# Two chained transformer blocks on one core: weight buffers in order of last use, later expert additions, and a softmax with negated minima whose division runs on GpSimd

## The chip, the cores and the metric

The kernel runs on one core of one Trainium2 chip. The metric is device microseconds (us) of one execution. Before the change the median of three runs was 2263.86 us (2260.80 to 2268.84).

Names of engines in the profile: PE is TensorE (matmul), PEld its weight load, DVE VectorE, ACT ScalarE, POOL GpSimd, SP the engine whose queue issues the weight transfers.

## The reference

`T` = 256 tokens of width 1024, float32. Block 1 has two layers of a mixer and an expert-choice FFN; block 2 has a token mixer (a gated linear recurrence and a long convolution) and a hierarchical mixture of 32 experts. What the change touches is block 1:

```python
def banked_softmax(s, sink):                  # s: scores + ALiBi bias + mask, per head
    m = max(s, axis=-1); m = maximum(m, sink) # sink only in the window attention
    p = exp(s - m)
    den = sum(p, axis=-1) + exp(sink - m)
    return (p / den) @ v

def hybrid_mixer(h):     # proj = h @ w_in; dilated: 4 heads x 3 dilations, window: 16 heads, 4 of keys
    g = sigmoid(gates + b_gate)
    return (g[0] * (dilated(q, k, v) @ w_a) + g[1] * (window(q, k, v, sink) @ w_b)) @ w_out

def expert_choice_ffn(h):                     # 16 experts, each takes its 32 best tokens
    aff = softmax(h @ w_router); gate, idx = top_k(aff.T, 32)
    ye = (silu(h[idx] @ w_gate) * (h[idx] @ w_up)) @ w_down
    return zeros.at[idx].add(gate * ye)
```

(Condensed; the dilated part combines its three dilations by their softmax denominators, which is one softmax over the concatenated 512 scores.)

## The kernel before

**Weights.** 745.8 MB of weights come from HBM, nearly all as chunks of 128 partitions x 2048 float32, 1 MB each. `Core.chunk` (L45) takes the next tag and `piece` (L57, DMA at L60) issues the transfer on SP into a buffer of that tag; `quarters` (L68) does it as four tiles of 512 columns. The tags are `w` (5 buffers), `x` (4 buffers), and the tiles of activations that are idle in that stage (`V`, `qa`, `qb`, `qc`, `ob`, `hgw`, `G`, `hn`, `hTa`). A fixed list, `K.ring`, with a running counter sets which tag is next; a list `K.spare` is used up ahead of it. SP issues in order, and a transfer waits until the last reader of its buffer is through. The compiler's scheduler fixes the order of instructions on each engine from the order in the program and its own model of time.

**Projections.** Matmuls of block 1's mixers and of block 2's token mixer are done as three passes (`mm3`, L118 to L120) over a high and a low part. `split` (L98, L99) makes them of a chunk's 512 columns: ACT copies the high part `wh`, then `wl` = chunk - `wh` is computed by DVE, or by POOL for every fourth. Layer 1's input projections but a last quarter are computed early, beside layer 0's expert down projections (class `Ahead`, whose generator `steps` gives 23 steps for each quarter of the model's width). Layer 1's mixer then has the last quarter of its projections (`pairs`, `rows`, added at L242), and the attention.

**Attention** (`mixer`, L318 on). For each head of a pair, the scores go to PSUM (`sc`, L436 dilated, L477 and L478 window), and DVE adds slope times distance and takes the running maximum (`ttr`, L423). `soften` (L405 to L420) negates the maximum (`nm`, L408, DVE), takes the exponential with the sum `den` (L411, ACT), adds the sink's term (L414 to L416), takes the reciprocal `r` (L418, DVE) and multiplies the probabilities `P` by it (L420, DVE). Then four transposes (L446, L484), a copy to `PT`, and the products with V (L454, L493). `P` and `PT` have four buffers each. `weave` interleaves these items with the projections: with `project_w` the dilated part, with the gates and the adaptive-norm products (`ada`, L565) the window part. `split_to` (L106, L107) writes the window output `ob`. The gates `Ga`, `Gb` are multiplied on POOL in layer 1 (L383).

**Experts** (L681 on). The router, the choice of tokens and a gather come first; then 16 experts' gate and up products (L774, 8 chunks each), and in four quarters `q` of the width, for four groups `y` of experts, the down products (L816, 4 chunks), the scaling `yd` (L109, L110), and the addition to `h`: four matmuls (L824) with the scatter matrix `Ge` and one DVE addition (L827). In layer 0, `ahead.steps` follow each addition from the second quarter on; in layer 1 pieces of `prep` (constants of block 2) stand between.

Of the kernel before, what the change touches and what calls it, by code (L numbers as in the profile page):

```python
# [19 lines left out]
L = 2  # L20
# [12 lines left out]
class Core:  # L33
    def __init__(self, ctx, tc, A):
# [57 lines left out]
    def split(self, src):  # L92
# [6 lines left out]
        (nc.gpsimd if n in self.idle or n % 4 == 3 else nc.vector).tensor_tensor(lo, src, hi.bitcast(F), OP.subtract)  # L99
# [111 lines left out]
class Ahead:  # L211
# [6 lines left out]
    def start(self):  # L218
# [5 lines left out]
        self.raw = K.t([128, 8, T], "raw", RING["x"], tag="x")  # L224

# [90 lines left out]
def mixer(K, h, l, ada, first=None, ahead=None):  # L316
    nc, A = K.nc, K.A
    if ahead:  # L318
        x = ahead.x
        ahead.turned(3)  # L320
    else:
# [1374 lines left out]
```

## Time and profile before

| | |
|---|---|
| runs (us) | 2260.80, 2263.86, 2268.84; median 2263.86 |
| profiled execution | 2264.96 us, span 2263.2 us, mean granted clock 0.906 |
| busy (us) | PE 1810.0, PEld 1026.7, DVE 786.9, ACT 588.7, POOL 220.7 |
| HBM | 745.77 MB read, 1.05 MB written; 330 GB/s over the span |

The profile comes from one execution. Its span is cut into stretches by stage: 70 to 215 us is layer 0's attention beside its own projections, 320 to 566 layer 0's gate and up products, 626 to 800 its down products beside layer 1's projections, 800 to 930 layer 1's attention, 985 to 1470 layer 1's experts, 1510 to 1700 block 2's token mixer, 1800 to 2263 its experts. Busy shares of one stretch, the bytes it moves, and what an engine waited for are read together; a share over the whole span mixes stages with different limits.

### The profile page before, as it was taken

Reading aid. Unit: us, or ns where it says so; the run is one execution under the profiler, and the core shown is the slowest. Engines: PE = TensorE matmul, PEld = TensorE weight load, DVE = VectorE, ACT = ScalarE, POOL = GpSimd, SP = SyncE. Lnnn points to the kernel's source line nnn. Section 1 sums busy time; section 2 is a strip of 40 time slices with the busy share of each in tenths; the row PEclk is TensorE's granted clock in tenths of the full one; section 3 lists DMA queues with packets and bytes.
Section 4 is the critical chain, followed back from the end, with each engine's and each line's share of the span. In section 5 each row is a group of like instructions: output and inputs, shape, how many; then the busy total and the mean of one; then the engine's idle time right before and its main releaser. Section 6 shows DMA issues by size and latency. Waiting matters only on the chain.

```text
span 2263.2 us, 30298 instructions
## 1 busy us (share of the span) xinstructions
PE 1810.0 (80%) x12172; PEld 1026.7 (45%) x12172; DVE 786.9 (35%) x1823; ACT 588.7 (26%) x1182; POOL 220.7 (10%) x179
## 2 busy tenths in 40 slices
PE   8999997666699998996778566669999877776765
PEld 8877741111277765842234223248888522121211
DVE  5766620000145589631211111147647511111112
ACT  5545510000033345620124200036325310000000
POOL 2111200000011122200000000024224100000000
PEclk9999997777799999998899777889999999999999
DMA  7446599999999944679999999982336799999996
GB/s 301 136 165 238 216 377 421 421 421 422 422 375 409 386 163 187 233 278 366 411 416 415 371 420 421 420 336 105 119 115 233 300 411 421 421 421 421 422 421 277
DMA packets 113626, 748.87 MB, mean 331 GB/s; under 512 B 14695, under 2 KB 15112, under 8 KB 25416
## 3 DMA queue, kind: packets, MB, share of 16 engines
q1 hardware_dynamic: 112936, 745.82, 81.7%
q8 instruction: 98, 1.61, 0.3%
q10 hardware_dynamic: 544, 1.05, 0.1%
q14 instruction: 48, 0.39, 0.1%
HBM read 745.77 MB, written 1.05 MB: 330 GB/s over the span
## 4 chain that ended last, share of the span: by engine, by line
PE 44%; DMA 27%; issue 21%; DVE 5%; ACT 2%; POOL 0%; POOLq 0%; SPq 0%; DVEq 0%; ACTq 0%
DMA w<-in_w_eg 15%; DMA w<-in_w_ed 7%; PE mm L118 7%; PE mm L120 7%; PE mm L119 6%; PE mm L774 4%; PE acc L816 4%; DMA w<-in_w2z 1%; DVE wl L99 1%; PE acc L493 1%; PE acc L901 1%; PE sc L841 1%; DMA w<-in_ada 1%; PE acc L1181 1%; PE sc L478 1%
## 5 line engine op out<-in xcount | busy, mean ns | idle before, releaser
L774 PE MATMUL mm<-w,xT 128*32 128x512 f32 x2048 | 325.0, 743 | 131.4 <-DMA w<-in_w_eg 131.3
L98 ACT ACTIVATE wh<-w 128x512 fp32r<-128x512 f32 x384 | 239.5, 630 | 314.5 <-PE mm L119 237.1
L118 PE MATMUL mm<-hTa,wh 128*128 128x256 f32 x960 | 282.5, 296 | 8.3 <-DVE qa L242 2.4
L120 PE MATMUL mm<-hTa,wl 128*128 128x256 f32 x960 | 276.4, 291 | 4.5 <-DVE wl L99 4.2
L119 PE MATMUL mm<-hTb,wh 128*128 128x256 f32 x960 | 274.4, 287 | 1.2 <-DVE hTb L1004 1.2
L99 DVE TENSOR_TENSOR wl<-w,wh 128x512 fp32r<-128x512 f32 x286 | 220.1, 775 | 100.4 <-ACT wh L98 97.5
L1429 PE MATMUL mm<-w,xT 128*32 128x512 f32 x1024 | 174.1, 618 | 61.5 <-DMA w<-in_w2eg 60.9
L99 POOL TENSOR_TENSOR wl<-w,wh 128x512 fp32r<-128x512 f32 x98 | 129.7, 1324 | 917.2 <-ACT wh L98 411.8
L774 PEld LDWEIGHTS mm<-w,xT 128*32 128x32 f32 x2048 | 59.1, 123 | 352.3 <-DMA w<-in_w_eg 245.3
L816 PE MATMUL acc<-w,hid 128*32 128x256 f32 x2048 | 167.0, 436 | 59.9 <-DMA w<-in_w_ed 59.9
L118 PEld LDWEIGHTS mm<-hTa,wh 128*128 128x128 f32 x960 | 182.8, 191 | 28.4 <-issue 13.5
L120 PEld LDWEIGHTS mm<-hTa,wl 128*128 128x128 f32 x960 | 182.5, 191 | 14.3 <-issue 6.2
L119 PEld LDWEIGHTS mm<-hTb,wh 128*128 128x128 f32 x960 | 183.5, 191 | 5.4 <-issue 2.4
L816 PEld LDWEIGHTS acc<-w,hid 128*32 128x32 f32 x2048 | 76.8, 124 | 136.2 <-DMA w<-in_w_ed 68.2
L1470 PE MATMUL acc<-w,work 128*32 128x512 f32 x512 | 103.4, 681 | 36.4 <-DMA w<-in_w2ed 35.0
L1429 PEld LDWEIGHTS mm<-w,xT 128*32 128x32 f32 x1024 | 33.6, 110 | 172.1 <-DMA w<-in_w2eg 126.1
L175 POOL TENSOR_TENSOR rs<-rs,mhalf 128x2 f32<-128x2 f32 x9 | 6.7, 748 | 1010.7 <-DVE rs L174 1010.5
L790 DVE TENSOR_TENSOR hid<-tp,sg 128x256 f32<-128x256 f32 x32 | 13.6, 424 | 221.0 <-ACT sg L789 221.0
L88 DVE COPY gs<-mm 128x512 f32<-128x512 f32 x16 | 11.1, 692 | 199.6 <-PE mm L774 199.6
L110 DVE SCALAR_TENSOR_TENSOR yd<-acc,gw,yd 128x256 fp32r<-128x256 f32 x32 | 15.5, 483 | 179.4 <-ACT yd L109 179.4
L789 ACT ACTIVATE sg<-tp 128x256 f32<-128x256 f32 x32 | 12.3, 383 | 227.5 <-PE tp L786 227.4
L109 ACT ACTIVATE yd<-acc,gw 128x256 fp32r<-128x256 f32 x32 | 15.1, 473 | 213.2 <-PE acc L816 213.2
(469 smaller groups left out, 2504.4 us busy)
## 6 DMA issues: line engine op xcount, KB each, us to landing
w<-in_w_eg SPq DMA_DIRECT2D x250, 1024.0 KB, 15.6
w<-in_w_ed SPq DMA_DIRECT2D x128, 1024.0 KB, 14.1
w<-in_w2eg SPq DMA_DIRECT2D x126, 1024.0 KB, 19.8
w<-in_w2ed SPq DMA_DIRECT2D x63, 1024.0 KB, 19.8
w<-in_ada SPq DMA_DIRECT2D x24, 1024.0 KB, 6.3
w<-in_w_in SPq DMA_DIRECT2D x22, 1024.0 KB, 7.1
w<-in_wk SPq DMA_DIRECT2D x20, 1024.0 KB, 9.3
w<-in_w_b SPq DMA_DIRECT2D x8, 1024.0 KB, 6.2
```

The costliest lines, as they stand in the source:

```text
L98: self.hi = nc.scalar.activation(hi, src, AF.Copy)
L99: (nc.gpsimd if n in self.idle or n % 4 == 3 else nc.vector).tensor_tensor(lo, src, hi.bitcast(F), OP.subtract)
L118: mm(out, lhsT=l[0], rhs=r[0], start=start, stop=False)
L119: mm(out, lhsT=l[0], rhs=r[1], start=False, stop=False)
L120: mm(out, lhsT=l[1], rhs=r[0], start=False, stop=stop)
L478: nc.tensor.matmul(p[:, sl], lhsT=q[hq], rhs=KL[hq, kv // 2, :], start=False, stop=True)
L493: nc.tensor.matmul(po[half * 64:half * 64 + 64, :T], lhsT=V[:, kt, c:c + 64], rhs=PTs[half][:, kt * 256:(kt + 1) * 256], start=(kt == 0), ...
L774: nc.tensor.matmul(gu[32 * j:32 * j + 32, :], lhsT=xT[:, k, (e % 8) * CAP:(e % 8 + 1) * CAP], rhs=w[:, j * 512:(j + 1) * 512], start=(k == ...
L816: nc.tensor.matmul(dn[32 * x:32 * x + 32, :T], lhsT=hid[e // 8][:, e % 8, f, hh * 32:hh * 32 + 32], rhs=ws[x][:, fb * T:(fb + 1) * T], sta ...
L841: nc.tensor.matmul(p[:, :T], lhsT=hn[:, tt, kb * 128:(kb + 1) * 128], rhs=oh[:, tt].rearrange("p a b -> p (a b)"), start=(tt == 0), stop=( ...
L1429: nc.tensor.matmul(gu[o:o + 32, :], lhsT=xT[:, k, y:y + CAP2], rhs=ws[x][:, (2 * kk + j) * 512:(2 * kk + j + 1) * 512], start=(k == 0), st ...
L1470: nc.tensor.matmul(dn[32 * x:32 * x + 32, :], lhsT=hid[x][:, c, :], rhs=wd[x][:, c * 512:(c + 1) * 512], start=(c == 0), stop=(c == 3), ti ...
```

## The change

1. The ring becomes a queue: `chunk` takes the first tag and puts it at the end; `take` and `give` remove and add buffers when a tile is used otherwise; a tag with "-" is used once.
2. In the experts' down loop the addition of a group comes later: after the next group's products, and in layer 0 from the second quarter on after six (or five) of the `ahead.steps`.
3. The scores are kept negated, so `ttr` takes minima and the exponential has scale -1 and the minimum as bias; the negation `nm` is gone.
4. A pair of heads shares the sink's addition and exponential, the denominator's addition and the reciprocal; the scores of the next pair are issued ahead of the transposes and products of this one (`overlapped`).
5. The division P * r runs on GpSimd (new lines L466 and L514) and no longer on DVE.
6. In layer 1's mixer every second `wl`, not every fourth, is POOL's (`K.share = 2`), until the window part is through.
7. A constant is shorter (`iota` 65 to 33), one is added (`nsink`), and `rtmp` shares a buffer.

```diff
-        self.ring, self.spare, self.idle = list("wwxwx"), [], ()
+        self.ring, self.spare, self.idle = list("wwxwxwxwx"), [], ()
...
     def chunk(self, src):
         tag = self.spare.pop(0) if self.spare else None
-        if tag is None:
-            tag = self.ring[self.nchunk % len(self.ring)]
-            self.nchunk += 1
         if isinstance(tag, tuple):
             return self.quarters(src, tag)
+        if tag is None:
+            tag = self.ring.pop(0)
+        if tag[0] == "-":
+            return self.piece(src, tag[1:])
+        self.ring.append(tag)
         return self.piece(src, tag)
+    def take(self, *tags):
+        for tag in tags:
+            self.ring.remove(tag)
+    def give(self, *tags):
+        self.ring += tags
...
-        (nc.gpsimd if n in self.idle or n % 4 == 3 else nc.vector).tensor_tensor(lo, src, hi.bitcast(F), OP.subtract)
+        (nc.gpsimd if n in self.idle or n % self.share == self.share - 1 else nc.vector).tensor_tensor(lo, src, hi.bitcast(F), OP.subtract)
...
-    def soften(P, n, m, extra=None):
-        nm = K.t([128, 4], "nm", 3)[:, :n]
-        nc.vector.tensor_scalar(nm, m, -1.0, None, op0=OP.mult)
...
-            nc.vector.tensor_scalar(P[:, i, :], P[:, i, :], r[:, i:i + 1], None, op0=OP.mult)
-    def ttr(P, s, neg, slope, init, m):
-        nc.vector.tensor_tensor_reduce(P, s, neg, slope, init, OP.add, OP.max, m)
+    def ttr(P, s, neg, slope, init, m):
+        nc.vector.tensor_tensor_reduce(P, s, neg, -slope, init, OP.add, OP.min, m)
+    def exponential(P, m, den):
+        last.append(nc.scalar.activation(P, P, AF.Exp, bias=m, scale=-1.0, accum_out=den))
+    def overlapped(items, begin, end):
+        before = None
+        for item in items:
+            now = begin(*item)
+            yield
+            if before:
+                yield from end(*before)
+            before = now
+        yield from end(*before)
...
+    def dilated_scores(pair, tt):
...
+        nc.vector.reciprocal(r[:, :2], den[:, :2])
+        for half in range(2):
+            nc.gpsimd.tensor_scalar(Ps[half], Ps[half], r[:, half:half + 1], None, op0=OP.mult)
+        return pair, tt, Ps
...
+    def window_scores(pair):
...
+        last.append(nc.scalar.activation(ex, ex, AF.Exp))
+        nc.vector.tensor_add(den, den, ex)
+        r = K.t([128, 4], "r", 3)
         nc.vector.reciprocal(r, den)
+        for i in range(4):
+            sl = slice(i % 2 * 256, i % 2 * 256 + 256)
+            nc.gpsimd.tensor_scalar(Ps[i // 2][:, sl], Ps[i // 2][:, sl], r[:, i:i + 1], None, op0=OP.mult)
+        return pair, Ps
...
     def window():
+        yield from overlapped(((pair,) for pair in range(8)), window_scores, window_values)
...
-    weave((project_w(), 5), (dilated(), 8))
-    weave((gates(), 8), (islice(ada, 5), 5), (window(), 20))
+    weave((project_w(), 5), (dilated(), 12))
+    if ahead:
+        K.give("x")
+    weave((gates(), 8), (islice(ada, 5), 5), (window(), 26))
+    K.share = 4
+    K.give("x", "x")
...
-    K.ring = list("wwxwx")
-    K.spare = [None] * 7 + ["V", "qa", "qb", "qc"] + ([] if ahead else ["ob"]) + ["hgw"] + (["G"] if ahead else [])
+    if ahead:
+        K.spare = [None] * 7 + ["V", "-qa", "qb", "qc", "-ob", "hgw", "G"]
+    else:
+        K.spare = [None] * 7 + ["-V", "-qa", "qb", "qc", "ob", "hgw"]
...
-            K.ring = ["w", "x", "w", "V", "w", "x", "qb", "w", "qc", "x", "w", "hgw", "x", "G"] if ahead else list("wwxwx") + ["qc"]
+        if not ahead and e == 3:
+            K.take("qb", "ob", "hgw", "hn", "x")
+        if e == 8:
+            K.give("hTa")
...
-    K.ring = ["w", "x", "w", "qc", "w", "x", "w", "x", "w"] if ahead else ["w", "x", "w", "qc", "w", "hTa", "x", "w", "qa", "w"]
+    if ahead:
+        K.take("hTa")
+    else:
+        K.give("qa")
...
+            if late:
+                add(*late)
             yd = K.t([128, 2, T], "yd", NP, tag="PT", dt=FR)
             K.split_to(yd[:, 0], yd[:, 1], dn[:, :T], gw[:, y:y + 1])
...
-            if ahead and q and y < 3:
-                for _ in islice(ahead.steps, (8, 8, 7)[y]):
+            late = (q, y, yd)
+            if ahead and q:
+                for _ in islice(ahead.steps, (6, 6, 6, 5)[y]):
                     pass
+                add(*late)
+                late = None
             elif not ahead:
                 next(prep, None)
-    K.ring = list("wwxwx")
+    if late:
+        add(*late)
...
-    K.spare = ["qa", "V", "qb", "G", "hgw", "x", "x", "ob", "x", "w", ("wh", "wh", "wh", "wl"),
+    K.spare = ["qa", "-V", "qb", "-G", "hgw", "x", "x", "ob", "x", "w", ("wh", "wh", "wh", "wl"),
                ("wl", "wl", "PT", "PT"), "qc", "w", "w", "w", "w"]
-    K.ring = ["qa", "w", "qb", "hgw", "w", "x", "ob", "w", "x", "qc", "w", "x", "w"]
+    K.ring = []
```

(In `experts`, `ahead` is set in layer 0, which feeds it; in `mixer` it is set in layer 1, which uses it. The `take` and `give` calls at the smaller places and the heads of the new functions are left out.)

How the order moves is shown at three places.

GpSimd in layer 1's mixer, from the first gate and key multiplications to the merging of the branches (`Ga`, `Gb` are the gates, `P` the probabilities, L539 before and L580 now the merge). Before:

```order
L378 TENSOR_TENSOR qa<-qa,qb 128x512
L378 TENSOR_TENSOR qb<-qb 128x512 x2
L99 TENSOR_TENSOR wl<-w,wh 128x512 x3
L383 TENSOR_TENSOR Ga<-Ga,qb 128x512 x3
L99 TENSOR_TENSOR wl<-w,wh 128x512
L383 TENSOR_TENSOR Ga<-Ga,qb 128x512
L383 TENSOR_TENSOR Gb<-Gb,qb 128x512 x4
L99 TENSOR_TENSOR wl<-w,wh 128x512 x2
L539 TENSOR_TENSOR Ga<-Ga,Gb 128x256 x2
```

Now, the second half of the same stretch:

```order
L466 TENSOR_SCALAR P<-P,r 128x512 x2
L397 TENSOR_TENSOR Ga<-Ga,qb 128x512 x4
L397 TENSOR_TENSOR Gb<-Gb,qb 128x512
L466 TENSOR_SCALAR P<-P,r 128x512 x2
L111 TENSOR_TENSOR wl<-w,wh 128x512 x2
L397 TENSOR_TENSOR Gb<-Gb,qb 128x512
L514 TENSOR_SCALAR P<-P,r 128x256 x4
L397 TENSOR_TENSOR Gb<-Gb,qb 128x512 x2
L514 TENSOR_SCALAR P<-P,r 128x256 x4
L111 TENSOR_TENSOR wl<-w,wh 128x512
L514 TENSOR_SCALAR P<-P,r 128x256 x24
L111 TENSOR_TENSOR wl<-w,wh 128x512
```

The divisions stand among the `wl` and the gates, 24 of the 32 narrow ones in one run at the end. In layer 0, whose mixer had only `wl` on this engine, they stand in groups of two to eight between single `wl`.

SP ahead of layer 0's experts (`in_ada` are the adaptive-norm weights, `in_w_eg` the gate and up weights; whole chunks are L60 before and L72 now, quarters L68 and L80). Before:

```order
L60 DMA w<-in_w_eg 128x2048 x2
L60 DMA w<-in_ada 128x2048
L60 DMA w<-in_w_eg 128x2048 x7
L68 DMA w_3379<-in_w_eg 128x512
...
L60 DMA w<-in_w_eg 128x2048 x15
```

Now:

```order
L72 DMA w<-in_w_eg 128x2048
L72 DMA w<-in_ada 128x2048
L72 DMA w<-in_w_eg 128x2048 x9
L80 DMA w_3259<-in_w_eg 128x512
...
L72 DMA w<-in_w_eg 128x2048 x15
```

With the three whole chunks that stand further up before, and also now, 12 of them were ahead of the first group of six quarters, and now 13 are.

TensorE at the end of layer 0's down loop (`acc<-w,hid` are down products, `sc<-yd,Ge` the addition, `mm` layer 1's projections). Before:

```order
L119 MATMUL mm<-wl,hTa 128x512
L120 MATMUL mm<-wh,hTb 128x512
L816 MATMUL acc<-w,hid 32x256 x30
L824 MATMUL sc<-yd,Ge_4314 128x256 x4
L190 MATMUL tp<-ident,h 128x128 x4
```

Now:

```order
L878 MATMUL acc<-w,hid 32x256 x29
L130 MATMUL mm<-wh,hTa 128x512 x2
L131 MATMUL mm<-wl,hTa 128x512
L132 MATMUL mm<-wh,hTb 128x512
L130 MATMUL mm<-wh,hTa 128x512
L131 MATMUL mm<-wl,hTa 128x512
L132 MATMUL mm<-wh,hTb 128x512
L130 MATMUL mm<-wh,hTa 128x512
L131 MATMUL mm<-wl,hTa 128x512
L132 MATMUL mm<-wh,hTb 128x512
L131 MATMUL mm<-wl,hTa 128x512
L132 MATMUL mm<-wh,hTb 128x512
```

Behind the last of these stands the addition, `L864 MATMUL sc<-yd,Ge_4188 128x256 x4`. Before, four of layer 0's additions from the second quarter on stood right behind their own down products (or behind three more); now one does, and the others have projections between. In layer 1 the last rows were 30 products and one addition (4 matmuls), and are now 63 products and two additions (8 matmuls).

## Rows read from the trace of the kernel before

**Rows 1.** The page, busy time by engine, and the chain that ended last.

```profile
PE 1810.0 (80%) x12172; PEld 1026.7 (45%) x12172; DVE 786.9 (35%) x1823; ACT 588.7 (26%) x1182; POOL 220.7 (10%) x179
...
PE 44%; DMA 27%; issue 21%; DVE 5%; ACT 2%; POOL 0%; POOLq 0%; SPq 0%; DVEq 0%; ACTq 0%
```

**Rows 2.** Busy time of each engine by stretch; the first line names the columns.

```profile
core 0: us, PE busy (x) PEld busy (x) DVE busy (x) ACT busy (x) POOL busy (x), PEclk, DMA share, GB/s
70.00:215.00 145.00, 145.00 (x1008) 114.91 (x1007) 102.15 (x343) 78.76 (x200) 16.76 (x13) 1.00 0.49 172
...
320.00:566.00 246.00, 164.57 (x944) 31.17 (x942) 11.07 (x22) 10.62 (x23) 0.00 (x0) 0.76 1.01 420
626.00:800.00 174.00, 167.94 (x1571) 130.18 (x1571) 90.09 (x140) 56.67 (x99) 23.62 (x18) 0.98 0.95 385
800.00:930.00 130.00, 116.09 (x710) 83.77 (x711) 111.53 (x359) 72.53 (x190) 25.92 (x19) 0.96 0.49 180
985.00:1060.00 75.00, 58.69 (x366) 25.20 (x358) 13.77 (x35) 7.80 (x15) 0.00 (x0) 0.88 0.86 338
...
1250.00:1330.00 80.00, 45.72 (x268) 12.64 (x268) 7.66 (x23) 11.92 (x17) 0.00 (x0) 0.70 0.94 385
1330.00:1470.00 140.00, 93.46 (x966) 44.44 (x966) 17.86 (x32) 7.73 (x17) 0.00 (x0) 0.80 1.01 421
...
1510.00:1700.00 190.00, 183.20 (x1320) 160.36 (x1320) 112.32 (x200) 82.76 (x145) 59.27 (x45) 0.99 0.32 120
1800.00:2240.00 440.00, 319.58 (x1775) 91.50 (x1774) 66.03 (x136) 31.58 (x59) 0.00 (x0) 0.95 1.01 416
```

**Rows 3.** Groups of VectorE by form, 800 to 930: layer 1's attention.

```profile
L99 DVE TENSOR_TENSOR wl<-w,wh 128x512 fp32r<-128x512 f32 x21 | 18.5, 879 | 0.4 <-ACT wh L98 0.2
...
L420 DVE TENSOR_SCALAR P<-P,r 128x256 f32<-128x256 f32 x32 | 10.9, 381 | 0.0
L364 DVE TENSOR_TENSOR q<-tq,q 64x256 fp32r<-64x256 f32 x16 | 9.3, 580 | 0.5
...
L420 DVE TENSOR_SCALAR P<-P,r 128x512 f32<-128x512 f32 x8 | 5.6, 700 | 0.1
...
L408 DVE TENSOR_SCALAR nm<-m 128x2 f32<-128x2 f32 x16 | 2.6, 162 | 0.0
L418 DVE RECIPROCAL r<-den 128x2 f32<-128x2 f32 x16 | 2.5, 158 | 0.0
L414 DVE TENSOR_TENSOR ex<-sink,nm 128x2 f32<-128x2 f32 x16 | 2.4, 152 | 0.0
L416 DVE TENSOR_TENSOR den<-den,ex 128x2 f32<-128x2 f32 x16 | 2.4, 153 | 0.1
```

**Rows 4.** Groups of VectorE by form, 70 to 215: layer 0's attention.

```profile
L99 DVE TENSOR_TENSOR wl<-w,wh 128x512 fp32r<-128x512 f32 x41 | 28.0, 686 | 3.1 <-ACT wh L98 2.8
...
L420 DVE TENSOR_SCALAR P<-P,r 128x256 f32<-128x256 f32 x32 | 9.8, 348 | 0.3
...
L364 DVE TENSOR_TENSOR q<-tq,q 64x256 fp32r<-64x256 f32 x16 | 6.7, 420 | 0.5
...
L420 DVE TENSOR_SCALAR P<-P,r 128x512 f32<-128x512 f32 x8 | 3.9, 483 | 0.2
```

**Rows 5.** Groups of GpSimd by form, whole run.

```profile
L99 POOL TENSOR_TENSOR wl<-w,wh 128x512 fp32r<-128x512 f32 x98 | 129.7, 1324 | 917.2 <-ACT wh L98 411.8 <-DVE qa L88 360.0 <-issue 30.5
...
L1047 POOL TENSOR_SCALAR z<-z,oml 128x256 f32<-128x256 f32 x8 | 9.0, 1122 | 10.5 <-ACT z L1026 10.4
```

**Rows 6.** Timeline, one moment of layer 1's attention (start us, us): GpSimd, then VectorE.

```profile
829.85 1.28 POOL L99 TENSOR_TENSOR wl<-w,wh 128x512 fp32r<-128x512 f32 x1 [6.99 <-ACT wh L98]
...
830.08 1.34 DVE L420 TENSOR_SCALAR P<-P,r 128x512 f32<-128x512 f32 x1
```

**Rows 7.** One tile's instructions: the window outputs ob, 870 to 930.

```profile
L107 DVE TENSOR_TENSOR ob<-acc,ob x8: 402/418/424, 889.8 to 927.0; 128x256 fp32r<-128x256 f32 x8
```

**Rows 8.** Waits of TensorE, 626 to 800 (us in total, times, longest).

```profile
PE sc L824 <- ACT yd L109: 2.5, 4, 0.6
```

More of the change, by code (lines that the diff above doesn't have):

```diff
@@ L224, in start @@
         self.raw = K.t([128, 8, T], "raw", RING["x"], tag="x")
+        K.take("V", "qb", "G", "hgw", "x")
     def dest(self, j):
@@ L320, in mixer @@
         ahead.turned(3)
+        K.share = 2
     else:
@@ new lines, in dilated_values @@
+    def dilated_values(pair, tt, Ps):
+        po, q = pos[pair], slice(tt * 128, tt * 128 + 128)
+        PTs = []
+        for P in Ps:
+            PTs.append(turned([P[:, j * 128:(j + 1) * 128] for j in range(4)]))
+            yield
+        for j, (g, kt) in enumerate(((0, 0), (0, 1), (1, tt), (2, tt))):
+            for half in range(2):
+                c = (4 * g + 2 * pair + half) * 64
+                nc.tensor.matmul(po[half * 64:half * 64 + 64, q], lhsT=V[:, kt, c:c + 64],
+                                 rhs=PTs[half][:, j * 128:(j + 1) * 128], start=(j == 0), stop=(j == 3))
+        if tt:
+            K.split_to(oa[0][:, pair, :], oa[1][:, pair, :], po)
@@ new lines, in window_values @@
+    def window_values(pair, Ps):
+        po = pos[pair % 2]
+        PTs = []
+        for P in Ps:
+            PTs.append(turned([P[:, tt * 256 + kt * 128:tt * 256 + kt * 128 + 128] for kt in range(2) for tt in range(2)]))
+            yield
+        for kt in range(2):
+            for half in range(2):
+                c = 768 + (pair // 4 * 2 + half) * 64
+                nc.tensor.matmul(po[half * 64:half * 64 + 64, :T], lhsT=V[:, kt, c:c + 64],
+                                 rhs=PTs[half][:, kt * 256:(kt + 1) * 256], start=(kt == 0), stop=(kt == 1))
+        K.split_to(ob[0][:, pair, :], ob[1][:, pair, :], po)
@@ L622, in first_loads @@
     K.sink, K.bgate = K.load("sink", [128, L, 16, 2]), K.load("bgate", [128, L, 16])
+    K.nsink = K.const.tile([128, L, 16, 2], F, name="nsink")
+    nc.vector.tensor_scalar(K.nsink, K.sink, -1.0, None, op0=OP.mult)
     K.gffn = K.load("gffn", [128, L, KD])
@@ L806, in experts, with add @@
             K.copy(Ge[-1].rearrange("p a b -> p (a b)"), p)
-    K.ring = ["w", "x", "w", "qc", "w", "x", "w", "x", "w"] if ahead else ["w", "x", "w", "qc", "w", "hTa", "x", "w", "qa", "w"]
+    if ahead:
+        K.take("hTa")
+    else:
+        K.give("qa")
+    def add(q, y, yd):
+        p = K.bank("sc")
+        for tt in range(2):
+            for i in range(2):
+                nc.tensor.matmul(p[:, tt * T:(tt + 1) * T], lhsT=Ge[y // 2][:, y % 2, tt * 128:(tt + 1) * 128],
+                                 rhs=yd[:, i], start=(i == 0), stop=(i == 1))
+        hs = h[:, :, q * T:(q + 1) * T]
+        nc.vector.tensor_add(hs, p.rearrange("p (t c) -> p t c", t=2), hs)
+    late = None
     for q in range(4):
```

148 lines of the change are left out of this document (57 added, 91 removed).

## The prediction

> **What bounds the kernel now.** I read the page first, then the span cut into stretches, then the groups of the one stretch where the vector engine leads, then single moments of it. TensorE is busy 1810 us and the chain that ended last is 44% TensorE and 27% DMA [rows 1]; VectorE, at 787 us, looks harmless. That is an average over stages with different limits, and the stretches take it apart [rows 2]:
>
> - Layer 0's attention (70 to 215): TensorE busy 145.0 of 145 us, VectorE 102, GpSimd 16.8. It is TensorE's.
> - Layer 0's experts (320 to 566): 420 GB/s with the DMA engines full. It is the weights'. The end of its down projections, filled with layer 1's projections (626 to 800), is TensorE's again, 167.9 of 174.
> - Layer 1's attention (800 to 930): its projections are already done, so little matmul work covers the softmax. VectorE 111.5 of 130, TensorE 116.1, GpSimd 25.9, DMA 180 GB/s. No engine is full; the work runs as a chain in which VectorE and TensorE alternate.
> - Layer 1's experts: 421 GB/s from 1330 to 1470, but 338 from 985 to 1060 and 385 from 1250 to 1330. Block 2's token mixer (1510 to 1700) is TensorE's, 183.2 of 190, and its experts (1800 to 2240) run at 416 GB/s.
>
> So instructions taken off VectorE can pay in one stretch of 130 us only, and ring order only where the DMA engines have gaps.
>
> **Softmax, layer 0.** The same edits as in layer 1 lighten VectorE by some 22 us, but TensorE has no idle time there [rows 2]: worth 0. The cover is TensorE's own work. It would be gone if TensorE had to wait for a `wl` that stands on GpSimd behind two to eight divisions (the order above). I bound that at 0 to +5 us: 35.9 + 13.6 us of divisions (priced below) beside the 16.8 that GpSimd does now make 66 of 145 us.
>
> **Softmax, layer 1.** Removed from VectorE: the 40 divisions, 10.9 + 5.6; the 24 negations, 2.6 and, for the 8 of one column, 8 × 0.162 = 1.3 at the mean of the others; half of the window's reciprocals, sink additions and denominator additions, 1.3, 1.2 and 1.2, and 4 of the dilated part's 8 reciprocals, 4 × 0.158 = 0.6 [rows 3]. That is 24.7 us. `share = 2` moves about 6 `wl` at 0.879, 5.3 us. Nothing is added but one instruction on 32 columns at the start.
>
> Added to GpSimd: 32 divisions of 256 columns. It has done this form already: L1047, 1.12 us [rows 5], three times VectorE's 0.348 [rows 4]; 35.9 us. For 512 columns no row exists: between 1.12 (all of it fixed) and 2.24 (all by column); I take 1.7, 8 of them 13.6 us. Six `wl` at 1.32 make 7.9 [rows 5]. GpSimd goes from 25.9 to 83.3 us of 130. The Trainium skill would have it cheaper ("GPSIMD Engine Reference", Engine selection: with one input GpSimd is about at line rate); at VectorE's 0.348 the pair-wide divisions would cost 11 us in place of 35.9. L1047 contradicts this, and the measured row decides.
>
> Then the two engines disturb each other. A GpSimd `wl` ran from 829.85 for 1.28 us; a VectorE division that began at 830.08 took 1.34 [rows 6], where in layer 0 the mean is 0.483 [rows 4]: it waited until the other was through. The same forms in both layers give the size [rows 3, 4]: 21 × (0.879 − 0.686) + 32 × (0.381 − 0.348) + 16 × (0.580 − 0.420) + 8 × (0.700 − 0.483) = 9.5 us lost in layer 1 beside 25.9 us of GpSimd. With 83.3 us of GpSimd, but only 17.0 us of such VectorE work left of 36.1 (15 `wl` × 0.686 + 16 × 0.420, against 21, 32, 16 and 8 at layer 0's means), I estimate 9.5 × 83.3/25.9 × 17.0/36.1 = 14.4. 5.5 of the 9.5 lie on what stays (15 × 0.193 + 16 × 0.160), so 8.9 come on top. VectorE: 111.5 − 24.7 − 5.3 + 8.9 = 90.4 us of 130.
>
> VectorE then stands well under TensorE's 116.1. The stretch can shrink by 130 − 116.1 = 13.9 at most, and by 0 if the chain through the engines only changes hands. I take half, **−7**. What is late next is TensorE itself, or GpSimd.
>
> The skill has a rule against this. "SBUF — State Buffer", Who interferes with whom, says that VectorE and GpSimd share one port pair as an exclusive lock, held for a whole instruction; "Perfetto Trace Analysis", Optimizing Scalar/DVE Operations, draws from it that moving work between these two may not help. By that, this term would be 0 and the sum below −5.9 instead of −12.9. The trace agrees on the lock [rows 6]; whether it eats all of the gain is rival 2.
>
> **Later additions.** TensorE waits four times for `yd` at the additions of layer 0, 2.5 us in all, 0.6 each [rows 8]. In the new order products of layer 1 stand ahead of all of them but one: 3 × 0.6 = **−1.9**. In layer 1 the down projections are the DMA's (421 GB/s [rows 2]): 0, but the last two additions now both follow the last product. That is four more matmuls and one addition at the end of the stage: **+1** (bounds 0 and 2, as products of 256 columns and one VectorE instruction of 512 are all it adds).
>
> **Ring.** One more megabyte of expert weights can start before layer 0's experts, on SP, ahead of the quarters (order above). At 420 GB/s [rows 2] 1.05 MB are **−2.5**. In layer 1's experts `hTa` joins the ring at expert 8, one more buffer of lead. What can be won there: 75 × (1 − 338/421) = 14.8 us and 80 × (1 − 385/421) = 6.8 [rows 2]. The first also holds the router and the gather ahead of the experts, which no ring shortens. One buffer covers one megabyte: **−2.5**, bounds 0 and −13.8 (half of the first, all of the second). Block 2's ring yields nearly the old order, and its stretch is at 416 GB/s: 0. The smaller constants and the shared `rtmp`: 0.
>
> **Sum:** −7 − 1.9 + 1 − 2.5 − 2.5 = −12.9. The profiled execution took 2264.96 us, 1.1 above the median of 2263.86; 2264.96 − 12.9 = **2252 us**.
>
> **Rivals.**
>
> 1. *GpSimd becomes the bound; slower.* Window outputs leave every (927.0 − 889.8)/7 = 5.3 us [rows 7]. Each pair of heads will need four divisions on GpSimd, 4 × 1.12 = 4.5. From 1.33 us each, GpSimd sets the pace. If each also waits for one VectorE `wl` (0.69 [rows 4]), it is 1.81, 7.2 us a pair: 8 × 1.9 = +15 in place of −7. With the other terms (−5.9): 2264.96 + 15 − 5.9 = 2274. For it: 4.5 is already 85% of the pace, and the `wl` and gate products queue between the divisions. Against it: six of the eight pairs follow each other on GpSimd with nothing between, and by then VectorE has few `wl` left.
> 2. *Nothing is left of it.* The lock and the longer path of each division (1.12 for 0.348) eat the softmax gain, and the transfers gain nothing either: 2264.96 − 1.9 + 1 = 2264, or 2259 with the ring. For it: VectorE and TensorE are both near full in layer 1, so a chain, not an engine, may set the time. Against it: the new order has two pairs in flight, which hides a longer division.
> 3. *All of it comes.* TensorE becomes the bound of layer 1's attention (−13.9) and the ring takes the gaps (−13.8): 2264.96 − 13.9 − 13.8 − 2.5 − 1.9 + 1 = 2234. For it: the gaps are there in the rows. Against it: one buffer more is little against 14.8 us.
>
> **How the numbers follow.** Forecast 0.46, rival 1 0.19, rival 2 0.21, rival 3 0.14. A measurement of this kernel tells about 0.3%, 6.8 us, from no change: faster is below 2257.1, slower above 2270.7. Faster: nearly all of the forecast's case (0.45) and rival 3 (0.14), 0.59. Same: rival 2 and the upper end of the forecast, 0.22. Slower: rival 1, 0.19. The forecast's own range, with the softmax term from −13.9 to 0, is 2245 to 2259. With rival 3's 2234, and rival 1 up to its 2274, the range is 2233 to 2274; the 2 in 10 left out are a rival 1 that also delays layer 0, and gaps that vanish wholly.
>
> **What would show it.** Right: layer 1's attention 5 to 10 us shorter with VectorE near 90 us and GpSimd near 83; divisions of 256 columns near 1.1 us; GB/s from 985 to 1060 and 1250 to 1330 a little up; one wait at the additions. Wrong: divisions above 1.3 us and window outputs over 5.3 us apart (rival 1); VectorE's `wl` above 1.1 us and the stretch as long as now (rival 2); the two gaps at 415 GB/s (rival 3).

## The result, and the profile after

The changed kernel takes 2326.9 us (median of 4 runs, 2325.25 to 2329.1) against 2262.4 us of the kernel before on the same chip: a ratio of 1.028, 95% interval 1.0258 to 1.0303. It is 64 us **slower**. The forecast was 2252 us in a range of 2233 to 2274; the measured time lies outside it and on the other side.

The page of the kernel after, the rows that answer to [rows 1] (busy time by engine, chain that ended last):

```profile
PE 1853.5 (80%) x12172; PEld 1047.4 (45%) x12172; DVE 756.5 (33%) x1634; ACT 592.8 (25%) x1168; POOL 314.4 (14%) x265
...
PE 47%; DMA 25%; issue 21%; DVE 4%; ACT 2%; SPq 0%; POOL 0%; POOLq 0%; DVEq 0%; ACTq 0%
```

The edit did what it says: VectorE has 189 instructions and 30 us less, GpSimd 86 instructions and 94 us more. TensorE has the same 12172 matmuls and is busy 43 us longer. A longer time for the same instructions is the first hint of where to look.

First, where the time is lost. Two tiles' rows give the moments at which the expert products start and end (columns: shortest, median and longest of one, then first and last start in us). Before, gate and up products, then down products:

```profile
L774 PE MATMUL mm<-w,xT x2048: 589/617/1063, 289.9 to 1328.7; 128*32 128x512 f32 x187
...
L816 PE MATMUL acc<-w,hid x2048: 376/379/636, 586.6 to 1482.5; 128*32 128x256 f32 x187
```

After:

```profile
L822 PE MATMUL mm<-w,xT x2048: 589/617/1063, 294.3 to 1381.0; 128*32 128x512 f32 x187
...
L878 PE MATMUL acc<-w,hid x2048: 376/379/637, 587.8 to 1546.9; 128*32 128x256 f32 x187
```

and layer 1's window outputs after, which answer to [rows 7]:

```profile
L119 DVE TENSOR_TENSOR ob<-acc,ob x8: 419/420/425, 890.9 to 953.8; 128x256 fp32r<-128x256 f32 x8
```

Layer 0's experts start 4.4 us late (294.3 for 289.9), of which 3.2 are made up when the down products start (587.8 for 586.6). The last window output of layer 1 is 26.8 us late (953.8 for 927.0), the last gate product 52.3 (1381.0 for 1328.7), the last down product 64.4 (1546.9 for 1482.5). From there on nothing changes; the span ends 64.1 late. Layer 0's last addition begins 4.6 us late (805.3 for 800.7). So some 22 us are lost in layer 1's mixer up to the last window output, and 38 in layer 1's experts.

The stretches of the kernel after (columns as in [rows 2]):

```profile
70.00:215.00 145.00, 145.00 (x977) 112.89 (x975) 87.06 (x245) 77.94 (x188) 61.15 (x53) 1.00 0.44 161
...
320.00:566.00 246.00, 161.96 (x929) 34.73 (x927) 12.15 (x24) 12.50 (x26) 0.00 (x0) 0.78 0.99 407
...
626.00:800.00 174.00, 170.21 (x1604) 128.06 (x1600) 87.35 (x137) 56.63 (x99) 22.34 (x17) 0.99 0.99 404
800.00:930.00 130.00, 120.47 (x617) 84.42 (x610) 87.75 (x240) 62.24 (x157) 69.19 (x57) 0.80 0.31 118
...
985.00:1060.00 75.00, 69.36 (x377) 35.99 (x379) 24.98 (x61) 19.42 (x38) 4.60 (x4) 0.93 0.69 259
...
1250.00:1330.00 80.00, 56.94 (x346) 25.83 (x348) 14.09 (x40) 34.36 (x42) 0.00 (x0) 0.77 0.89 356
1330.00:1470.00 140.00, 79.80 (x726) 33.52 (x722) 12.30 (x23) 5.94 (x14) 0.00 (x0) 0.74 0.94 385
```

The stretch from 800 to 930 held all of layer 1's attention before, and now ends ahead of its last window outputs. From layer 0's last addition to the last window output, before and then after:

```profile
800.70:927.50 126.80, 112.97 (x686) 80.85 (x687) 110.59 (x357) 71.14 (x188) 25.47 (x18) 0.96 0.48 179
...
805.30:954.30 149.00, 137.89 (x695) 92.61 (x694) 94.96 (x264) 72.07 (x182) 75.82 (x65) 0.77 0.36 135
```

VectorE went from 110.6 to 95.0 us, 15.6 less, where the forecast had 21.1 less (111.5 to 90.4). TensorE went from 113.0 to 137.9 us with about as many matmuls: its granted clock (the share of full speed at which it ran; 1.00 is 2.4 GHz, 0.50 is 1.2 GHz) is 0.77 there, and was 0.96. In layer 1's experts the transfers run at 385 GB/s from 1330 to 1470, where they ran at 421 [rows 2], and at 356 where they ran at 385.

The attention in slices of 10 us, kernel after:

```profile
870.00:880.00 10.00, 9.56 (x58) 7.60 (x57) 5.65 (x17) 4.63 (x16) 9.67 (x9) 0.83 0.31 107
880.00:890.00 10.00, 8.66 (x45) 5.72 (x44) 6.42 (x14) 4.59 (x13) 7.43 (x7) 0.85 0.28 105
890.00:900.00 10.00, 8.88 (x25) 4.76 (x25) 3.31 (x13) 3.46 (x11) 3.63 (x4) 0.50 0.32 106
900.00:910.00 10.00, 10.00 (x30) 5.64 (x29) 4.07 (x16) 3.39 (x12) 3.63 (x4) 0.50 0.00 1
910.00:920.00 10.00, 9.43 (x27) 4.92 (x25) 3.32 (x14) 3.21 (x11) 3.63 (x4) 0.50 0.00 0
...
930.00:940.00 10.00, 8.41 (x26) 4.17 (x24) 3.06 (x12) 3.94 (x12) 3.63 (x4) 0.50 0.41 123
940.00:950.00 10.00, 10.00 (x62) 4.84 (x61) 3.95 (x10) 6.09 (x12) 3.63 (x4) 0.75 0.97 385
950.00:960.00 10.00, 10.00 (x78) 8.81 (x77) 6.47 (x12) 5.05 (x10) 2.03 (x2) 1.00 1.03 402
```

and before:

```profile
890.00:900.00 10.00, 10.00 (x47) 5.70 (x47) 8.16 (x41) 6.16 (x24) 0.00 (x0) 1.00 0.02 10
900.00:910.00 10.00, 10.00 (x52) 6.11 (x50) 9.05 (x49) 6.43 (x25) 0.00 (x0) 1.00 0.01 2
910.00:920.00 10.00, 8.32 (x41) 5.03 (x42) 8.02 (x38) 8.04 (x24) 0.00 (x0) 0.86 0.73 259
```

At about 884 us, in both kernels, the projections that stand beside the window attention run out. From 890 to 910 the kernel before has TensorE at full clock (1.00, 2.4 GHz) with 47 and 52 matmuls in 10 us, and at 0.86 in the next 10 us; the kernel after is at 0.50 (1.2 GHz) with 25 to 30, and stays there until about 945. Window outputs leave every 9.0 us, (953.8 − 890.9)/7, and not every 5.3. TensorE looks nearly full all the while (8.4 to 10 of 10 us): a busy share says nothing here without the clock beside it.

GpSimd's groups after (L514 the window's division, L466 the dilated part's):

```profile
L514 POOL TENSOR_SCALAR P<-P,r 128x256 f32<-128x256 f32 x64 | 60.3, 960 | 59.6 <-DVE r L511 49.8 <-PE tp L441 9.3 <-ACT wh L110 0.4
L466 POOL TENSOR_SCALAR P<-P,r 128x512 f32<-128x512 f32 x16 | 26.8, 1688 | 15.8 <-DVE r L464 8.5 <-PE mm L132 5.4 <-ACT q L376 2.0
```

The divisions cost what was estimated or less: 0.96 us for 1.12, 1.69 for 1.7. In the tail GpSimd is busy 3.63 of 10 us: it is not full.

What TensorE waits for from 880 to 945, after (us in total, times, longest): its longest entry among the matmuls, and the one entry in which the transposes' weight loads wait for GpSimd:

```profile
PE sc L499 <- DVE m L421: 2.7, 5, 1.0
...
PEld tp L441 <- POOL P L514: 1.5, 2, 0.8
```

All of the matmuls' named waits come to 4.7 us, and none is for GpSimd. At 0.50 TensorE is thus busy nearly all the time and has no long wait for the division; what the division has to do with the clock is left to the experiments.

### The profile page after: what moved, and what is told of

Same layout as the page of the kernel before. It is cut to its first block, busy times and chain, and to the rows that moved or that the text cites. A ratio compares the mean times of both kernels' runs of the same rounds, so it can differ in the third digit from the quotient of the medians.

```text
span 2327.3 us, 30221 instructions
## 1 busy us (share of the span) xinstructions
PE 1853.5 (80%) x12172; PEld 1047.4 (45%) x12172; DVE 756.5 (33%) x1634; ACT 592.8 (25%) x1168; POOL 314.4 (14%) x265
## 4 chain that ended last, share of the span: by engine, by line
PE 47%; DMA 25%; issue 21%; DVE 4%; ACT 2%; SPq 0%; POOL 0%; POOLq 0%; DVEq 0%; ACTq 0%
DMA w<-in_w_eg 15%; DMA w<-in_w_ed 8%; PE mm L130 7%; PE mm L132 7%; PE mm L131 7%; PE mm L822 5%; PE acc L878 5%; PE acc L526 1%; PE sc L905 1%; PE tp L441 1%; PE acc L965 1%; PE sc L500 1%; PE acc L606 1%; PE acc L1245 1%; DVE wl L111 1%
## 5 line engine op out<-in xcount | busy, mean ns | idle before, releaser
L822 PE MATMUL mm<-w,xT 128*32 128x512 f32 x2048 | 332.1, 747 | 144.7 <-DMA w<-in_w_eg 144.3
L111 POOL TENSOR_TENSOR wl<-w,wh 128x512 fp32r<-128x512 f32 x104 | 137.6, 1324 | 793.1 <-ACT wh L110 742.7
L878 PE MATMUL acc<-w,hid 128*32 128x256 f32 x2048 | 176.3, 438 | 84.2 <-DMA w<-in_w_ed 84.2
L1493 PE MATMUL mm<-w,xT 128*32 128x512 f32 x1024 | 184.9, 651 | 62.7 <-DMA w<-in_w2eg 62.3
L1534 PE MATMUL acc<-w,work 128*32 128x512 f32 x512 | 98.2, 645 | 37.3 <-DMA w<-in_w2ed 35.9
L96 ACT ACTIVATE gs<-mm 128x512 f32<-128x512 f32 x16 | 9.6, 597 | 233.8 <-PE mm L822 210.7
```

The source lines that it names most:

```text
L111: (nc.gpsimd if n in self.idle or n % self.share == self.share - 1 else nc.vector).tensor_tensor(lo, src, hi.bitcast(F), OP.subtract)
L822: nc.tensor.matmul(gu[32 * j:32 * j + 32, :], lhsT=xT[:, k, (e % 8) * CAP:(e % 8 + 1) * CAP], rhs=w[:, j * 512:(j + 1) * 512], start=(k == ...
L878: nc.tensor.matmul(dn[32 * x:32 * x + 32, :T], lhsT=hid[e // 8][:, e % 8, f, hh * 32:hh * 32 + 32], rhs=ws[x][:, fb * T:(fb + 1) * T], sta ...
L1493: nc.tensor.matmul(gu[o:o + 32, :], lhsT=xT[:, k, y:y + CAP2], rhs=ws[x][:, (2 * kk + j) * 512:(2 * kk + j + 1) * 512], start=(k == 0), st ...
L1534: nc.tensor.matmul(dn[32 * x:32 * x + 32, :], lhsT=hid[x][:, c, :], rhs=wd[x][:, c * 512:(c + 1) * 512], start=(c == 0), stop=(c == 3), ti ...
```

## The experiments

**Theory 1** from these rows: two separate losses, the softmax part through TensorE's clock, and the ring. Its rival: one loss, in which the slow attention starves the experts after it. Of e1 to e6 and e10 to e14 there is one time each, so of those only differences of several us are read; the kernel before, timed beside them, took 2263 to 2270 us.

**e1: ring and later additions alone.** The changed kernel with the kernel before's `soften`, `ttr`, `dilated` and `window` put back, and every fourth `wl` on GpSimd again.

```diff
-    weave((project_w(), 5), (dilated(), 12))
+    weave((project_w(), 5), (dilated(), 8))
...
-    weave((gates(), 8), (islice(ada, 5), 5), (window(), 26))
+    weave((gates(), 8), (islice(ada, 5), 5), (window(), 20))
...
-            nc.gpsimd.tensor_scalar(Ps[i // 2][:, sl], Ps[i // 2][:, sl], r[:, i:i + 1], None, op0=OP.mult)
+            nc.vector.tensor_scalar(P[:, i, :], P[:, i, :], r[:, i:i + 1], None, op0=OP.mult)
```

> The kernel before with the new ring and the later additions; softmax, division and weave as before. Theory 1 (two separate losses: about 27 us in layer 1's attention from the softmax part, where TensorE's granted clock falls to 0.5, and about 37 us in layer 1's experts from the ring): 2290 to 2305 us, window outputs of layer 1 done near 927 us as before, granted clock 0.9 or more from 880 to 926, and the DMA rate from 1060 to 1470 near 385 GB/s. Rival (one loss: the slow attention starves the experts after it, the ring itself is harmless): 2255 to 2268 us.

Measured 2303.1 us (2265.6 for the kernel before beside it), last window output at 923.3 us. Two stretches, 900 to 920 and 1060 to 1470, and the second of them in the kernel before:

```profile
900.00:920.00 20.00, 18.02 (x108) 10.26 (x109) 14.37 (x68) 14.83 (x49) 0.00 (x0) 1.00 0.51 177
...
1060.00:1470.00 410.00, 265.23 (x1792) 111.22 (x1792) 49.56 (x114) 74.30 (x109) 0.70 (x1) 0.77 0.93 379
```

```profile
1060.00:1470.00 410.00, 286.56 (x2048) 120.28 (x2048) 59.61 (x137) 74.53 (x113) 0.69 (x1) 0.83 1.00 411
```

Full clock in the attention, 379 GB/s in the experts for 411: with nothing slow ahead of it the ring, with the later additions, loses 37 us. The rival falls.

**e2: softmax part alone.** Ring and additions as before.

```diff
-        if tag is None:
-            tag = self.ring.pop(0)
-        if tag[0] == "-":
-            return self.piece(src, tag[1:])
-        self.ring.append(tag)
+            tag = self.ring[self.nchunk % len(self.ring)]
+            self.nchunk += 1
...
-            late = (q, y, yd)
```

> The kernel before with the softmax part of the change alone (negated minima, pairs, overlap, division on GpSimd, weave numbers, share of wl); ring and additions as before. Theory 1: 2285 to 2295 us, window outputs of layer 1 done 20 to 30 us later than before, granted clock near 0.5 in the tail, and the experts' stage as long as before. Rival: about 2320 us, as the experts starve here too.

Measured 2287.0 us, last window output at 951.8 us (before 927.0). From 900 to 920:

```profile
900.00:920.00 20.00, 19.33 (x52) 10.10 (x52) 6.67 (x28) 7.05 (x25) 7.24 (x8) 0.50 0.00 1
```

The clock is at 0.50 without the new ring. The two parts nearly add up: 37.5 + 21.4 = 59 of the 64 us.

**e3: old ring**, softmax and additions as changed. The edit is the first hunk of e2's, with the old lists, and not the second.

> The changed kernel with the old ring (fixed lists and counter); softmax and later additions as changed. Theory 1: 2285 to 2295 us, as e2, since the later additions are worth little. If the additions cost in the experts' down stage, 2300 us or more with TensorE's products out of step there.

Measured 2270.7 us: less than expected, 16 below e2. The later additions, which e2 lacks, gain; layer 0's `h` is complete at 796 us here and at 805 in e2 (before: 801), which is 9 of the 16. Expert products as long as before. e9 takes this up.

**e4: division on VectorE** in the changed kernel.

```diff
-            nc.gpsimd.tensor_scalar(Ps[half], Ps[half], r[:, half:half + 1], None, op0=OP.mult)
+            nc.vector.tensor_scalar(Ps[half], Ps[half], r[:, half:half + 1], None, op0=OP.mult)
...
-            nc.gpsimd.tensor_scalar(Ps[i // 2][:, sl], Ps[i // 2][:, sl], r[:, i:i + 1], None, op0=OP.mult)
+            nc.vector.tensor_scalar(Ps[i // 2][:, sl], Ps[i // 2][:, sl], r[:, i:i + 1], None, op0=OP.mult)
```

> The changed kernel with the 80 divisions back on VectorE. If the division on GpSimd is what makes layer 1's attention slow: about 2300 us, granted clock 0.9 or more in the tail, window outputs every 5.3 us or less. If the overlap of pairs or the weave does it: clock still 0.5 in the tail and 2320 to 2330 us.

Measured 2305.9 us, clock 0.91 or more in each 20 us from 880 to 940, window outputs from 885.2 to 923.9 us. Of the softmax part, the division's engine is what costs 21 us; overlap, pairs, minima and weave are not.

**What is wrong with the ring.** Reading on from e1: the queue `K.ring` now lives on from stage to stage. Layer 0's experts put `qc` into it (a tag without "-"), nothing takes it out, and layer 1's experts put it in again. The tag has one buffer. Places among SP's transfers, in the order of the program, of the transfers into that buffer late in layer 1's experts:

```
kernel before    433 440 447 451 457 465 471 475
changed kernel   433 440 445 452 455 457 466 472 477 479
e5 below         431 441 448 457 467 477
```

Before, they stand 4 to 8 places apart. In the changed kernel some stand 2 or 3 apart; the second then has to wait until TensorE has read the first, and all behind it on SP wait too. No view shows this wait, as buffer numbers are left out there; e5 tests it by its price. SP's order was on record in the rows of the order, but without its buffers.

**e5: `qc` once.** Theory 2: that double entry is the ring's loss.

```diff
     K.take("x", "x")
+    if ahead:
+        K.take("qc")
```

> The changed kernel, but the tag of the buffer qc is taken out of the ring when layer 1's mixer takes that buffer, so that it stands in the ring once and not twice in layer 1's experts. Theory 2 (the ring's 37 us come from two entries for one buffer: its transfers follow each other 2 to 9 places apart and hold SP's queue): 2288 to 2298 us, and the DMA rate from 1060 to 1470 near 410 GB/s or more. Rival (the order of last use itself, a whole ring that turns over in groups of four, costs it): above 2315 us.

Measured 2286.4 us, 41 below the changed kernel, just under the range expected:

```profile
1060.00:1470.00 410.00, 295.15 (x1958) 119.21 (x1958) 58.68 (x134) 76.90 (x114) 0.70 (x1) 0.82 0.98 404
```

The double entry was most of it. Some of the 41 came in the attention, whose outputs run from 889.9 to 943.5 us here, so the ring's own share is nearer 30 (e8 gives a cleaner number).

**e6: more work for TensorE**, otherwise the changed kernel. Eight more score products for each pair of heads in layer 1, which the right ones overwrite.

```diff
+                for _ in range(2 if ahead else 0):
+                    nc.tensor.matmul(p[:, sl], lhsT=q, rhs=KK[:, half, kv // 2, :], start=True, stop=True)
                 nc.tensor.matmul(p[:, sl], lhsT=q, rhs=KK[:, half, kv // 2, :], start=True, stop=False)
```

> The changed kernel with eight more score products for each pair of heads in layer 1's window attention, overwritten by the right ones. It only adds work to TensorE. If the loss there is TensorE's granted clock, which falls because TensorE does too little between its waits: clock above 0.8 from 890 to 940, window outputs of layer 1 done 10 to 25 us earlier than in the changed kernel (954 us), 2302 to 2318 us in all. If the loss is GpSimd's pace or the wait for the division: 10 to 15 us longer, 2335 to 2345 us, with the clock low.

Measured 2320.0 us, 7 less than without the added work and 2 above the range expected. The window outputs run from 892.2 to 938.8 us, 47 us in place of 63:

```profile
900.00:920.00 20.00, 18.89 (x96) 11.69 (x96) 9.29 (x39) 9.98 (x33) 10.89 (x12) 1.00 0.00 1
```

More work, done sooner, at clock 1.00: the clock is a price of its own.

**e7 and e8: both losses removed.** e7 is e3 with e4's edit; e8 is e5 with e4's edit.

> The changed kernel with the old ring and with the divisions on VectorE. If the two losses are separate: 2270.7 - 21 = 2250 us, faster than both kernels; what is left are the later additions and the smaller softmax operations. If the 16 us between e2 and e3 were chance of the order: 2258 to 2266 us.

> The changed kernel with qc once in the ring and with the divisions on VectorE. Theory 2: 2250 to 2265 us, as e7 but with the order of last use. Rival: above 2290 us.

e7: median 2260.0 us (ten runs, 2255.4 to 2281.5), ratio to the kernel before 0.9993 (0.9961 to 1.0025): no difference. e8: 2270.9 us, 1.0029 (1.0013 to 1.0045): a little slower. The 2250 us expected of e7 were missed; it lies in the other range, by which the 16 us between e2 and e3 were chance of the order.

The runs now price each loss beside different partners. The double entry costs 41 us with the division on GpSimd (changed kernel, e5) and 35 with it on VectorE, where the attention is fast either way (e4, e8). The division costs 21 us in the changed kernel, 15 with `qc` once (e5, e8) and 11 with the old ring (e3, e7). Both losses are there without the other, as theory 1 had it, but they are not simply added. e8 came out 6 us above its range. Its layer 0 ends 7 us later than e7's (last addition at 803.3 us for 796.4), and its last down product in layer 1 starts 161 us after the first (1327.6 to 1488.6), e7's 152 us (1325.0 to 1476.9). What of the order of last use costs the 11 us between them I did not settle.

**e9: later additions alone**, on the kernel before.

```diff
+            if late:
+                add(*late)
...
-            if ahead and q and y < 3:
-                for _ in islice(ahead.steps, (8, 8, 7)[y]):
+            late = (q, y, yd)
+            if ahead and q:
+                for _ in islice(ahead.steps, (6, 6, 6, 5)[y]):
                     pass
+                add(*late)
+                late = None
```

> The kernel before with the later additions alone. If they are what e7 has over the kernel before (layer 0 ended 5 us earlier there, the rest was level): 2257 to 2261 us, h of layer 0 complete near 796 us in place of 801. If the 5 us came from the smaller softmax operations in layer 0: no change, 2262 to 2266 us. If only the new order of the whole matters: h near 801.

Median 2255.2 us (six runs, 2246.9 to 2255.5), ratio 0.9963 (0.995 to 0.9977): **0.4% faster than the kernel before**, by 8 us at the median, and 2 below the range expected. TensorE from 626 us until `h` is nearly done; the profiled execution was the one of 2246.9 us, 8 below the other five:

```profile
626.00:787.00 161.00, 161.00 (x1544) 124.32 (x1544) 84.36 (x131) 53.62 (x94) 22.29 (x17) 1.00 0.98 404
```

No idle time at all, where 6 us of a slightly longer stretch were idle before [rows 2]; no wait at an addition is left in it.

**e10: half of the divisions.** e3 with the pair's second head on VectorE.

```diff
-            nc.gpsimd.tensor_scalar(Ps[i // 2][:, sl], Ps[i // 2][:, sl], r[:, i:i + 1], None, op0=OP.mult)
+            (nc.vector if i // 2 else nc.gpsimd).tensor_scalar(Ps[i // 2][:, sl], Ps[i // 2][:, sl], r[:, i:i + 1], None, op0=OP.mult)
```

> As e3 (old ring, later additions, new softmax), with the division of a pair's second head on VectorE and of its first on GpSimd. If the wait for the division is what lowers TensorE's clock: the wait is half as long, clock 0.85 or more from 890 to 920, window outputs of layer 1 done 10 to 20 us earlier than in e3 (941 us), 2255 to 2262 us. If any use of GpSimd there lowers it: clock near 0.5 and 2268 to 2272 us.

Measured 2265.0 us, 3 above the range expected. Outputs from 883.7 to 925.7 us, 42 us between e3's 58 and e7's 35, with the clock at 0.85:

```profile
900.00:920.00 20.00, 16.73 (x85) 12.05 (x83) 13.30 (x47) 13.66 (x41) 7.26 (x8) 0.85 0.47 175
```

**e11: e6's added products on e3.**

> As e3, with the eight overwritten score products for each pair of layer 1's window attention, as in e6. If the clock is the price and the ring no longer hides the gain: clock 1.0 from 900 to 940, window outputs done 8 to 15 us earlier than in e3 (941 us), and the total down by as much, 2256 to 2264 us. If the products cost what the clock gives back: 2268 to 2275 us.

Measured 2285.1 us, 14 more than e3, and outside what either side expected. Outputs from 885.9 to 948.2 us:

```profile
900.00:920.00 20.00, 20.00 (x60) 12.14 (x58) 6.45 (x26) 6.20 (x21) 7.24 (x8) 0.50 0.00 0
```

The same products beside which the clock stayed up in e6 did not keep it up here, and then they only add work at half clock. With e6 it makes a pair with the same window code: 47 us at clock 1.00, 62 us where it fell to 0.50. Adding work is no remedy, and it left open why the clock falls.

**e12: fewer `wl` on GpSimd.** e7 without `K.share = 2`.

```diff
-        K.share = 2
```

> As e7 (old ring, divisions on VectorE), with every fourth wl on GpSimd in layer 1's mixer, as before, and not every second. If moving six wl off VectorE is worth their 0.88 us each: 3 to 6 us longer than e7 in layer 1's attention (window outputs done at 924 to 927 us in place of 921). If contention eats it: level, 919 to 922 us.

Measured 2259.8 us, last window output at 922.5 us for e7's 920.6: level. The six `wl` were worth nothing that can be told.

**e13 and e14: wait or work?** Both on e3. e13 lets GpSimd write its quotients to a tile that nothing reads; e14 leaves the divisions out.

```diff
+            to = K.t([128, T], "side", 2, tag="Ge") if ahead else Ps[i // 2][:, sl]
-            nc.gpsimd.tensor_scalar(Ps[i // 2][:, sl], Ps[i // 2][:, sl], r[:, i:i + 1], None, op0=OP.mult)
+            nc.gpsimd.tensor_scalar(to, Ps[i // 2][:, sl], r[:, i:i + 1], None, op0=OP.mult)
```

```diff
+            if not ahead:
+                nc.gpsimd.tensor_scalar(Ps[i // 2][:, sl], Ps[i // 2][:, sl], r[:, i:i + 1], None, op0=OP.mult)
-            nc.gpsimd.tensor_scalar(Ps[i // 2][:, sl], Ps[i // 2][:, sl], r[:, i:i + 1], None, op0=OP.mult)
```

> As e3 (old ring, division on GpSimd), but in layer 1's window attention GpSimd writes the divided probabilities to a tile that nothing reads, so the transposes take the undivided ones: the division is left out of the result there, GpSimd's work and its use of memory stay, only the wait for it is gone. If waiting for the division lowers TensorE's clock: clock 0.9 or more from 890 to 920, and from the first to the last window output of layer 1 34 to 40 us in place of e3's 58. If GpSimd's work beside the other engines does it: clock near 0.5 and 55 us or more.

> As e3, with the 32 divisions of layer 1's window attention left out altogether. Both theories: clock 0.9 or more and 32 to 38 us from the first to the last window output. If the clock still falls, neither wait nor work of the division is the cause, but the overlap of pairs or the order.

e13 measured 2256.7 us, e14 2253.2 us (the kernel before beside them 2269.9). The window outputs of e13, and its stretch from 900 to 920:

```profile
L109 DVE TENSOR_TENSOR ob<-acc,ob x8: 421/424/426, 877.5 to 916.7; 128x256 fp32r<-128x256 f32 x8
```

```profile
900.00:920.00 20.00, 18.02 (x97) 11.65 (x98) 12.86 (x45) 14.31 (x39) 11.71 (x13) 1.00 0.52 192
```

and of e14:

```profile
L109 DVE TENSOR_TENSOR ob<-acc,ob x8: 414/419/419, 883.4 to 916.6; 128x256 fp32r<-128x256 f32 x8
```

GpSimd does the same 32 divisions, but with nobody waiting for them the clock stays at 1.00 and the outputs take 39 us in place of 58. It is the wait, and not GpSimd's work: that costs at most the 6 us between e13 and e14 (33 us). e13 and e14 also free the transposes of the sum and the reciprocal; e4 and e7, which keep these, are fast too. What is not separated from the wait is the order that the scheduler makes with it: TensorE's transposes stand in runs of eight in e7, and in runs of one, three or four in e3. Such short runs alone do not lower the clock, as e13 has them too.

## Why the prediction was wrong

**Softmax, layer 1** (−7; from layer 0's last addition to the last window output, +20 in e2 and +22 in the changed kernel). The step that failed is "by 0 if the chain through the engines only changes hands": the forecast took 0 as its worst case, and only rival 1 went beyond it (+15). The terms before it held in the main. VectorE came to 95.0 us over the whole attention (90.4 foreseen) and GpSimd to 75.8 (83.3), the divisions were priced right, and GpSimd did not become the bound: rival 1's point, 1.33 us for a division, was not reached (0.96). So rival 1 found the right sign by the wrong mechanism. I counted how full each engine is, and said in the same breath that no engine is full and a chain sets the time. In a chain what counts is the length of each link: a pair's four divisions took four times 0.38 us [rows 3] and now take 3.6 us in one piece (4 × 0.91), ahead of the transposes. TensorE then had fewer matmuls in the same time (40 and 41 in 10 us in e5 while its clock was still up, for 47 and 52 before), its granted clock fell to 0.50, and at 1.2 GHz TensorE itself became the long link. e7 and e13 show it from both sides: VectorE's division, or GpSimd's with no one waiting, keep 1.00 from 900 to 920. How the fewer matmuls bring the clock down is not shown.

The rule weighed in the prediction, that moving work between VectorE and GpSimd may not help ("Perfetto Trace Analysis", Optimizing Scalar/DVE Operations, in the Trainium skill), was right that nothing is gained. The reason that it gives, the shared port, was not what decided: VectorE's `wl` takes 0.919 us from 800 to 930 after and 0.879 before [rows 3], but 0.780 in e13, which keeps GpSimd's divisions, and there the window outputs take 39 us, near the 37 before.

```profile
L111 DVE TENSOR_TENSOR wl<-w,wh 128x512 fp32r<-128x512 f32 x16 | 14.7, 919 | 0.1
```

**Ring** (−2.5 in layer 1; measured +37 in e1 together with the later additions, and +46 in e4 against e7, 35 of it the double entry). The step that failed is "`hTa` joins the ring at expert 8, one more buffer of lead": I read what is added to the queue and not what was left in it from layer 0. The lists of before could not hold a stale entry, as each stage wrote its own; the queue could. Followed by hand from layer 0's experts to layer 1's, `qc` would have been seen twice. The chance that a ring is worse than the old one was not among the rivals at all. The other ring term held: layer 0's gate and up stage is 293.5 us long for 296.7 (from the first gate product to the first down product), −3.2 where −2.5 was foreseen.

**Softmax, layer 0** (0, bounds 0 to +5). Inside its bounds: TensorE is busy 145.0 of 145 us again, with VectorE's 15 us less (22 foreseen) and GpSimd's 44 us more beside it, and the experts start 4.4 us late. That is hardly told from 0: e3 and e14, whose layer 0 is the same, start them at 290.7 and 294.3.

**Later additions** (−1.9; −8 alone, at e9's median). Right sign, too small. I summed the waits that the view names at the additions, 2.5 us, and not the idle time of the stretch, 6 us. Beside the new ring that idle time is 3.8 us (174 − 170.2), and in e9's trace it is gone; as this trace is of the one fastest execution, what the 8 us at the median consist of is not shown. The +1 for the end of layer 1 does not show.

**The sum** was thus wrong through two terms, of some 20 us and of 37 or more, each held at 0 on its bad side although no row said so; only for the first did a rival go further. Two of its figures are slightly off and change nothing: the four contention terms add up to 9.4 us and not 9.5, and half of 14.8 with all of 6.8 is 14.2 and not 13.8.

## What to carry to other kernels

A queue of buffers that lives across stages has to be written out at every stage: one tag too many for one buffer cost more here (35 us) than the rest of the new order (11 us), as SP's queue, which issues in order, holds everything behind it. An operation on a chain that feeds TensorE is to be priced by the wait it adds there, and the price has a second part, here the larger one, the clock; look at granted clock and matmuls in 10 us, not at busy share. Test the parts of a change one by one: here a part worth 0.4% was buried under two others, and the whole came out 2.8% slower.

## What the hardware showed that I had not expected

TensorE at 1.2 GHz did not get its clock back although it was busy 8.4 to 10 of every 10 us from 890 to 940, with 25 to 30 matmuls in each. It came back at about 945, after one run of adaptive-norm products and as the output projections began (62 and 78 matmuls in 10 us):

```profile
940.51 5.01 PE L606 MATMUL acc<-w,cs 128*32 128x512 f32 x24
```

Small things decide here: the same added products went with 1.00 in e6 and not in e11, and e5, whose window code is the changed kernel's, stayed at full clock until nearly 910, where the changed kernel was at 0.50 from 890:

```profile
890.00:900.00 10.00, 8.62 (x40) 4.79 (x40) 5.47 (x24) 4.91 (x18) 7.04 (x8) 1.00 0.21 87
900.00:910.00 10.00, 8.98 (x41) 5.02 (x38) 5.69 (x24) 6.19 (x21) 5.31 (x7) 0.98 0.01 2
910.00:920.00 10.00, 9.43 (x26) 4.59 (x24) 2.48 (x9) 3.19 (x11) 2.12 (x3) 0.50 0.00 0
```

This also splits the price. At full clock, with the division on GpSimd, e5's first four window outputs leave from 889.9 to 905.4 us, 5.2 us apart and no slower than before (5.3), though by its matmuls, 40 and 41 in 10 us for 47 and 52, TensorE already does less; from there to the last, at 943.5, they are 9.5 us apart. In these rows most of the loss comes with the clock, and little with the longer division itself.
